# Seven block products instead of eight for gate and up in two of four feed-forwards of an fp32 encoder on one Trainium2 core

## The chip, the cores and the metric

One core of a Trainium2 chip runs the whole program. The metric is the device time of one execution in microseconds (us). The engines are TensorE (PE in the profile; PEld is its weight load), VectorE (DVE), ScalarE (ACT), GpSimd (POOL) and SyncE (SP), which issues the loads of weights.

## The reference

A trunk of two layers. Each layer is feed-forward, mixer, feed-forward, and every part is added to the residual x (512 tokens by 1024 features, float32):

```
x = x + 0.5 * swiglu(rms_norm(x, g1), w_gate, w_up, w_down)
x = x + mixer(rms_norm(x, g2))
x = x + 0.5 * swiglu(rms_norm(x, g3), w_gate, w_up, w_down)
swiglu(y) = (silu(y @ w_gate) * (y @ w_up)) @ w_down     # 1024 -> 2816 -> 1024
```

The change touches the first feed-forward (layer 0, before the mixer) and the last (layer 1, after it). The mixers (attention and a Fourier part in layer 0, latent attention and a state space part in layer 1) stay as they are.

## The kernel before

Activations lie transposed: x[c] holds features 128c to 128c+127 by 512 tokens, eight such tiles. Every fp32 operand of a product is split into a high and a low part in the type float32r (ScalarE copies the high part, VectorE subtracts it for the low part), and a product is the sum of three matmuls hi·hi, hi·lo and lo·hi (`mm3`, line 145; each is issued for 256 tokens at a time).

F = 2816 is 22 blocks of 128. A *unit* of weights is gate and up of one block: 128 partitions by 2048 columns, 1 MB, loaded by SP into one of three `raw` buffers (`load`), and split into `w_hi` (line 49, ScalarE) and `w_lo` (line 50, VectorE), two buffers each (`split`, `part`). A unit costs TensorE 8 feature blocks × 2 (gate, up) × 3 × 2 halves of the tokens = 96 matmuls of 128x128 by 256 columns, into the banks `pg` and `pu`. Behind it VectorE and ScalarE form the gate (lines 253 to 262): gn = pg · rows (255), sg = silu(gn) (257), un = pu · rows (259), a = sg · un (261), ah (154), al (161). `rows` holds each token's inverse root mean square, so that the norm is applied after the product; its columns come from squares of x by TensorE (`ms_cols`), a reciprocal root by Newton steps of 128x4 on VectorE (`rsqrt`, lines 205 to 218), and transposes on TensorE (`rows`). The down projection of 11 blocks at a time follows (two halves, `HF`), with one VectorE operation per chunk into x (line 298).

The tokens enter as `xg[c]`, x times the gain, split (`scale_split`), made chunk by chunk as the part before finishes x (`prep`). `side` is a generator of table operations (rope tables and others) of which one piece is emitted per unit.

The program is written unit by unit; a scheduler then fixes one static order per engine, and tiles from pools make a writer wait until the last reader of the buffer is done. Each engine works through its own list in order, so an operation that waits holds all that stand behind it in that list.

## Time and profile before

| what | value |
|---|---|
| median of 3 runs | 1852.09 us (1851.97 to 1856.15) |
| profiled execution | 1853.05 us, of which 1851.3 is the span of the trace |
| TensorE busy | 1830.1 us (99%), 15608 instructions |
| VectorE busy | 986.0 us (53%) |
| ScalarE busy | 622.6 us (34%) |

The span is the time from the first to the last instruction of the trace; the rest of the profiled execution lies around it. Busy shares are means over the whole program: what a stretch is bound by is read from that stretch.

### The profile page before, as it was taken

The page shows a single profiled execution, that of the slowest core. Times are in us where ns is not written, and L with a number is a line of the kernel's source. Part 1 is how long each engine was busy: PE and PEld are TensorE (multiplying, and loading weights), DVE is VectorE, ACT ScalarE, POOL GpSimd, SP SyncE. Part 2 cuts the span into 40 slices and gives each one's busy share as a digit, 9 for nine tenths or more (in the row PEclk, how much of TensorE's full clock was granted, in tenths as well). Part 3 has the DMA queues.
Part 4 walks back from the last instruction along what each step waited for, and adds up shares of the span by engine and source line. Part 5 has one row for each costly group of instructions (what it writes and reads, how often), then busy time and mean ns, then how long its engine had stood idle before and what let it go on. Part 6 is the DMA issues. An engine that isn't in the chain of part 4 may idle for free.

```text
span 1851.3 us, 35303 instructions
## 1 busy us (share of the span) xinstructions
PE 1830.1 (99%) x15608; PEld 1810.8 (98%) x15608; DVE 986.0 (53%) x1732; ACT 622.6 (34%) x818; POOL 85.4 (5%) x138
## 2 busy tenths in 40 slices
PE   9999999999999999999999999999989999999999
PEld 9999999999799999999999999999988899999999
DVE  5643444456955954556744434444688654434442
ACT  4321222324953222222332222223366632212321
POOL 0000000011120000000000000000045100000000
PEclk9999999999999999999999999999999999999999
DMA  6223221331122325342322233223144222133221
GB/s 209 93 73 121 95 105 64 117 108 68 37 92 92 113 100 150 112 111 100 128 103 92 79 116 110 89 73 109 69 129 141 79 96 103 64 118 113 85 89 67
DMA packets 63447, 185.65 MB, mean 100 GB/s; under 512 B 27424, under 2 KB 28352, under 8 KB 51136
## 3 DMA queue, kind: packets, MB, share of 16 engines
q1 hardware_dynamic: 63296, 183.41, 29.3%
q8 instruction: 122, 2.00, 0.4%
q14 instruction: 29, 0.24, 0.0%
HBM read 170.79 MB, written 10.49 MB: 98 GB/s over the span
## 4 chain that ended last, share of the span: by engine, by line
PE 95%; DVE 2%; ACT 1%; DMA 1%; issue 0%; POOL 0%; SPq 0%; ACTq 0%; POOLq 0%; DVEq 0%
PE pd L145 30%; PE pu L145 27%; PE pg L145 26%; PE pz L145 4%; PE etp L1447 1%; PE sc L145 1%; PE pf L145 1%; PE pql L145 1%; PE s_py L1230 1%; PE pq L145 1%; PE po L1467 0%; PE po L1468 0%; DVE et_lo L1459 0%; PE sc L533 0%; ACT e L1440 0%
## 5 line engine op out<-in xcount | busy, mean ns | idle before, releaser
L49 ACT ACTIVATE w_hi<-w_raw 128x2048 fp32r<-128x2048 f32 (+4 forms) x175 | 288.6, 1649 | 878.3 <-PE pu L145 449.7
L50 DVE TENSOR_TENSOR w_lo<-w_raw,w_hi 128x2048 fp32r<-128x2048 f32 (+4 forms) x172 | 338.2, 1966 | 166.2 <-ACT w_hi L49 166.0
L145 PE MATMUL pu<-xgh,w_hi 128*128 128x256 f32 x1440 | 282.9, 278 | 0.0
L145 PE MATMUL pu<-xgh,w_lo 128*128 128x256 f32 x1440 | 282.8, 278 | 0.0
L145 PE MATMUL pu<-xgl,w_hi 128*128 128x256 f32 x1440 | 282.6, 278 | 0.0
L145 PE MATMUL pg<-xgh,w_hi 128*128 128x256 f32 x1408 | 277.9, 279 | 1.2 <-ACT w_hi L49 1.2
L145 PE MATMUL pd<-al,w_hi 128*128 128x256 f32 x1408 | 277.5, 277 | 0.0
L145 PE MATMUL pd<-ah,w_lo 128*128 128x256 f32 x1408 | 277.4, 277 | 0.0
L145 PE MATMUL pd<-ah,w_hi 128*128 128x256 f32 x1408 | 276.7, 277 | 0.0
L145 PE MATMUL pg<-xgh,w_lo 128*128 128x256 f32 x1408 | 276.5, 278 | 0.0
L145 PE MATMUL pg<-xgl,w_hi 128*128 128x256 f32 x1408 | 276.4, 278 | 0.0
L145 PEld LDWEIGHTS pu<-xgh,w_hi 128*128 128x128 f32 x1440 | 218.7, 189 | 0.0
L145 PEld LDWEIGHTS pu<-xgh,w_lo 128*128 128x128 f32 x1440 | 218.2, 188 | 0.2 <-DVE w_lo L50 0.2
L145 PEld LDWEIGHTS pu<-xgl,w_hi 128*128 128x128 f32 x1440 | 218.2, 188 | 0.0
L145 PEld LDWEIGHTS pg<-xgh,w_hi 128*128 128x128 f32 x1408 | 213.8, 189 | 1.5 <-ACT w_hi L49 1.5
L145 PEld LDWEIGHTS pd<-ah,w_lo 128*128 128x128 f32 x1408 | 213.9, 188 | 0.0
L145 PEld LDWEIGHTS pd<-ah,w_hi 128*128 128x128 f32 x1408 | 213.6, 188 | 0.0
L145 PEld LDWEIGHTS pg<-xgl,w_hi 128*128 128x128 f32 x1408 | 213.4, 188 | 0.0
L145 PEld LDWEIGHTS pg<-xgh,w_lo 128*128 128x128 f32 x1408 | 213.4, 188 | 0.0
L145 PEld LDWEIGHTS pd<-al,w_hi 128*128 128x128 f32 x1408 | 213.4, 188 | 0.0
L255 DVE TENSOR_TENSOR gn<-pg,rows 128x512 f32<-128x512 f32 x88 | 60.7, 689 | 279.3 <-PE pg L145 279.3
L298 DVE SCALAR_TENSOR_TENSOR x<-pd,x 128x512 f32<-128x512 f32 (+1 forms) x65 | 44.4, 684 | 232.5 <-PE pd L145 232.5
(365 smaller groups left out, 2088.6 us busy)
## 6 DMA issues: line engine op xcount, KB each, us to landing
w_raw<-wa SPq DMA_DIRECT2D x86, 1024.0 KB, 4.9
w_raw<-wb SPq DMA_DIRECT2D x64, 704.0 KB, 4.0
w_raw<-we_qkv SPq DMA_DIRECT2D x6, 1024.0 KB, 4.9
w_raw<-we_out SPq DMA_DIRECT2D x3, 768.0 KB, 4.2
w_raw<-wo_out SPq DMA_DIRECT2D x3, 768.0 KB, 4.1
x<-xT SPq DMA_DIRECT2D x8, 256.0 KB, 5.5
dr_h<-s_h SPq DMA_DIRECT2D x8, 256.0 KB, 2.8
dr_g<-s_g SPq DMA_DIRECT2D x8, 256.0 KB, 3.0
```

The costliest lines, as they stand in the source:

```text
L49: self.nc.scalar.activation(hi, raw, AF.Copy)
L50: (self.eng or self.nc.vector).tensor_tensor(out=lo, in0=raw, in1=f32(hi), op=ALU.subtract)
L145: mm(out[:, c], lhs[l], rhs[r][:, c], start=first and i == 0 and j == 0, stop=last and i == 2, skip_group_check=len(cs) > 1)
L255: nc.vector.tensor_tensor(out=gn, in0=pg, in1=rstd, op=ALU.mult)
L298: nc.vector.scalar_tensor_tensor(out=x, in0=p, scalar=0.5, in1=x, op0=ALU.mult, op1=ALU.add)
L1230: nc.tensor.matmul(py[half][:, k, :], m[i][:, i4, :], r[:, k, :], start=i == 0, stop=i == 2)
L1447: nc.tensor.transpose(p[:, kc, :], e[:, kc * 128:kc * 128 + 128], T.ident)
```

## The change

Gate and up of a block are a product of a 256-column weight block (two halves of 128: gate and up) with 1024 features, and the tokens come in two halves of 256. Features are taken in two interleaved halves. So the product is a 2 by 2 block product: (gate, up) × (feature halves) × (token halves), eight block products. Strassen's scheme, in Winograd's form, gets by with seven, made from sums of weights and sums of tokens. A block product is here 4 feature blocks × 3 = 12 matmuls of 256 columns (`product`).

* Weights: g1 and g2 are the two halves of the gate's rows, u1 and u2 those of up's. The sums are s3 = g1 + u1 and s1 = u2 + u1 (one VectorE operation of 1024 columns, in place in `raw`), s2 = g1 + s1 and s4 = g2 + s2 (512 columns each); up comes out with its sign turned, which the -0.5 below sets right. g1, g2, s3, s1 lie in one tile of 2048 columns, which is split as before; s2, s4 and u2 are split apart (512 each). For this SP loads 1.5 MB per unit instead of 1 MB, in five pieces.
* Tokens: t1 to t4 are sums of the four blocks b11, b12, b21, b22, made once per feed-forward (`forms`), with two new copies with gain (y1, y2), and split.
* Order of a unit: g1·b11 (copied from the bank by ScalarE), s1·t1 (copied), then u2·t4 of the unit before it (copied, and its gate follows), s2·t2 accumulated on the first (copied), g2·b21, s4·b22, then gt's add on VectorE, s3·t3 accumulated (copied), and ut's add. Five bank copies of 256 columns by ScalarE and two adds by VectorE are new; `un` is gone: up's scale is applied behind the down projection, with the factor -0.5 (`rows` makes both).
* In the first feed-forward the first three of the 22 units stay as before, and t1 to t4 are made beside them. In the last feed-forward all 22 are new; t1 to t4 are made as the odd mixer finishes x (`prep_forms`).
* F is worked in three groups of 8, 7 and 7 blocks instead of two of 11, in these two feed-forwards; the chunk's addition into x is two VectorE operations.
* 60 slots of 512 columns become 66.

```diff
+GROUPS = (8, 7, 7)
...
     def load(self, i):
...
         raw = self.pool.tile([128, n], F32, tag="raw", name="w_raw", bufs=3)
-        for c in self.cuts(i, n):
-            self.nc.sync.dma_start(raw[:, c], src[:, c])
+        dma = self.nc.sync.dma_start
+        if slot:
+            self.u2[i] = slot("w_u2"), slot("w_u1")
+            dma(raw[:, 1024:1536], src[:, 0:512])
+            dma(raw[:, 1536:2048], src[:, 1536:2048])
+            dma(raw[:, 0:1024], src[:, 0:1024])
+            dma(self.u2[i][0], src[:, 1536:2048])
+            dma(self.u2[i][1], src[:, 1024:1536])
...
     def split(self, i):
...
+        if slot:
+            s = raw[:, 1024:2048].rearrange("p (a b) -> p a b", a=2)
+            self.nc.vector.tensor_tensor(out=s, in0=s, in1=self.u2[i][1][:, None, :].to_broadcast([128, 2, 512]), op=ALU.add)
         hi = self.pool.tile([128, n], F32R, tag="hi", name="w_hi")
         lo = self.pool.tile([128, n], F32R, tag="lo", name="w_lo")
         for c in self.cuts(i, n):
             self.part(raw[:, c], hi[:, c], lo[:, c])
-        self.ready[i] = (hi, lo)
+        self.ready[i] = self.forms(i, raw, hi, lo, slot) if slot else (hi, lo)
+    def forms(self, i, raw, hi, lo, slot):
+        add = self.nc.vector.tensor_tensor
+        out = {n: (hi[:, o:o + 512], lo[:, o:o + 512]) for n, o in (("g1", 0), ("g2", 512), ("s3", 1024), ("s1", 1536))}
+        s2, s4 = slot("w_s2"), slot("w_s4")
+        add(out=s2, in0=raw[:, 0:512], in1=raw[:, 1536:2048], op=ALU.add)
+        add(out=s4, in0=raw[:, 512:1024], in1=s2, op=ALU.add)
+        for n, f in (("s2", s2), ("s4", s4), ("u2", self.u2.pop(i)[0])):
+            out[n] = slot(n + "h", F32R), slot(n + "l", F32R)
+            self.part(f, *out[n])
...
+    def forms(self, j, norm, plain=None):
+        nc, v = self.nc, self.nc.vector
...
+        y1, y2 = self.slot("y1"), self.slot("y2")
+        for i, y in enumerate((y1, y2)):
+            g = norm * KD + 2 * j + i
+            nc.scalar.activation(y, self.x[2 * j + i], AF.Copy, scale=self.gains[:, g:g + 1])
+        b11, b12, b21, b22 = y1[:, 0:256], y1[:, 256:512], y2[:, 0:256], y2[:, 256:512]
+        ta, tb = self.slot("ta"), self.slot("tb")
+        t1, t2, t3, t4 = ta[:, 0:256], ta[:, 256:512], tb[:, 0:256], tb[:, 256:512]
+        v.tensor_tensor(out=t1, in0=b11, in1=b12, op=ALU.subtract)
+        v.scalar_tensor_tensor(out=t2, in0=t1, scalar=-1.0, in1=b22, op0=ALU.mult, op1=ALU.subtract)
+        v.tensor_tensor(out=t3, in0=b22, in1=b12, op=ALU.subtract)
+        v.scalar_tensor_tensor(out=t4, in0=t2, scalar=-1.0, in1=b21, op0=ALU.mult, op1=ALU.subtract)
+        if plain:
+            p1, p2 = plain
+        else:
+            q = self.slot("b1", F32R, (128, 2, 256))
+            nc.scalar.activation(q[:, 0], b11, AF.Copy)
+            v.tensor_tensor(out=q[:, 1], in0=b11, in1=f32(q[:, 0]), op=ALU.subtract)
+            p1, p2 = (q[:, 0], q[:, 1]), self.split(y2, "b2")
+        pa, pb = self.split(ta, "ta"), self.split(tb, "tb")
...
+    def product(self, out, w, n, first, last):
+        for k in range(KD // 2):
+            x = self.tf[n][k]
+            for i, (l, r) in enumerate(((0, 0), (0, 1), (1, 0))):
+                self.nc.tensor.matmul(out, w[l][:, k * 128:k * 128 + 128], x[r], start=first and k == 0 and i == 0,
+                                      stop=last and k == 3 and i == 2, skip_group_check=True)
+    def ffn_s(self, after, side=iter(()), plain=0, norm=0, ends=False):
...
+        def finish(sg_in, up):
+            gn = self.slot("gn")
+            tt(out=gn, in0=sg_in, in1=st["rows"], op=ALU.mult)
+            nc.scalar.activation(gn, gn, AF.Silu)
+            h = self.slot("a")
+            if up[1]:
+                nc.vector.scalar_tensor_tensor(out=h, in0=gn, scalar=-1.0, in1=up[0], op0=ALU.mult, op1=ALU.mult)
+            else:
+                tt(out=h, in0=gn, in1=up[0], op=ALU.mult)
+            act.append(self.split(h, "a"))
...
+        def last_product(u):
...
+            self.product(pb[:, a], w["u2"], "t4", False, True)
+            nc.scalar.activation(ut[:, a], pb[:, a], AF.Copy)
+            wait.append((gt, (ut, False)))
+            flush()
+        def unit(prev):
+            w = self.W.next()
+            pb, pc = self.bank("pg"), self.bank("pu")
+            gt, ut = self.slot("gt"), self.slot("ut")
+            copy = nc.scalar.activation
+            self.product(pb[:, a], w["g1"], "b11", True, False)
+            copy(gt[:, a], pb[:, a], AF.Copy)
+            self.product(pc[:, b], w["s1"], "t1", True, False)
+            copy(ut[:, a], pc[:, b], AF.Copy)
+            last_product(prev)
+            self.product(pb[:, a], w["s2"], "t2", False, False)
+            copy(gt[:, b], pb[:, a], AF.Copy)
+            self.product(pc[:, a], w["g2"], "b21", False, True)
+            self.product(pc[:, b], w["s4"], "b22", False, True)
+            tt(out=gt, in0=gt, in1=pc, op=ALU.add)
+            self.product(pb[:, a], w["s3"], "t3", False, False)
+            copy(ut[:, b], pb[:, a], AF.Copy)
+            tt(out=ut[:, b], in0=ut[:, b], in1=ut[:, a], op=ALU.add)
+            return {"w": w, "pb": pb, "gt": gt, "ut": ut}
...
+                if plain and f <= plain:
+                    for j in ((), (0,), (1, 2, 3))[f - 1]:
+                        self.forms(j, norm, (self.xg[2 * j], self.xg[2 * j + 1]))
...
+                def out(c, p, ts=slice(0, S)):
+                    t, x = self.slot("dn")[:, ts], self.x[c][:, ts]
+                    tt(out=t, in0=p, in1=st["down"][:, ts], op=ALU.mult)
+                    tt(out=x, in0=x, in1=t, op=ALU.add)
...
-    T.ffn_units(0, 1)
+    T.ffn_s_units(0, 1, 3)
...
-    T.ffn_units(1, 2)
+    T.ffn_s_units(1, 2)
     T.start(0)
-    T.ffn(prep(1), tables(), 1)
+    T.ffn_s(prep(1), tables(), 3)
...
-    T.odd_mixer(prep(5))
-    T.ffn(None, ends=True)
+    T.odd_mixer(lambda c: T.prep_forms(c, 5))
+    T.ffn_s(None, ends=True)
```

What the scheduler makes of it, at three places.

Place 1, VectorE in the first feed-forward, from the subtraction behind the reciprocal root, before (a gate of one pending unit, then the next unit's):

```order
L50 TENSOR_TENSOR w_lo_580<-w_raw_430,w_hi_579 128x2048
L255 TENSOR_TENSOR gn_541<-pg_169,rows_539 128x512
L259 TENSOR_TENSOR un_545<-pu_170,rows_539 128x512
L261 TENSOR_TENSOR a_547<-sg_543,un_545 128x512
L161 TENSOR_TENSOR al_551<-a_547,ah_549 128x512
L255 TENSOR_TENSOR gn_553<-pg_303,rows_539 128x512
```

The same place in the change (w_lo_681 is the low part of the second converted unit; gn to al belong to the three plain units; ta and tb hold the token sums t1, t2 and t3, t4, tal and tbl their low parts):

```order
L63 TENSOR_TENSOR w_lo_681<-w_raw_454,w_hi_680 128x2048
L405 TENSOR_TENSOR gn_590<-pg_169,rows_586 128x512
L409 SCALAR_TENSOR_TENSOR a_593<-gn_590,pu_170 128x512
L189 TENSOR_TENSOR al_597<-a_593,ah_595 128x512
L405 TENSOR_TENSOR gn_599<-pg_309,rows_586 128x512
L409 SCALAR_TENSOR_TENSOR a_602<-gn_599,pu_310 128x512
L189 TENSOR_TENSOR al_606<-a_602,ah_604 128x512
L405 TENSOR_TENSOR gn_608<-pg_483,rows_586 128x512
L409 SCALAR_TENSOR_TENSOR a_611<-gn_608,pu_484 128x512
L189 TENSOR_TENSOR al_615<-a_611,ah_613 128x512
L239 TENSOR_TENSOR ta_621<-y1_617 128x256
L240 SCALAR_TENSOR_TENSOR ta_621<-ta_621,y2_618 128x256
```

Before, the gates of pending units were followed by nothing that TensorE needs at once; in the change the token sums of the second pair (ta_621) stand behind all three gates.

Place 2, VectorE in the middle of the first feed-forward, before (one unit's whole list):

```order
L255 TENSOR_TENSOR gn_1218<-pg_1120,rows_539 128x512
L259 TENSOR_TENSOR un_1222<-pu_1121,rows_539 128x512
L50 TENSOR_TENSOR w_lo_1233<-w_raw_1114,w_hi_1232 128x2048
L261 TENSOR_TENSOR a_1224<-sg_1220,un_1222 128x512
L161 TENSOR_TENSOR al_1228<-a_1224,ah_1226 128x512
```

in the change (it makes the sums s2 and s4, and gt_2131 is the add to a bank copy):

```order
L464 TENSOR_TENSOR gt_2131<-gt_2131,pu_2130 128x512
L411 TENSOR_TENSOR a_2175<-gn_2172,ut_1999 128x512
L63 TENSOR_TENSOR w_lo_2243<-w_raw_2100,w_hi_2242 128x2048
L467 TENSOR_TENSOR ut_2132<-ut_2132 128x256
L189 TENSOR_TENSOR al_2179<-a_2175,ah_2177 128x512
L81 TENSOR_TENSOR w_s2_2246<-w_raw_2100 128x512
L69 TENSOR_TENSOR w_raw_2233<-w_raw_2233,w_u1_2235 128x1024
L82 TENSOR_TENSOR w_s4_2247<-w_raw_2100,w_s2_2246 128x512
L63 TENSOR_TENSOR s2l_2251<-w_s2_2246,s2h_2250 128x512
L63 TENSOR_TENSOR s4l_2255<-w_s4_2247,s4h_2254 128x512
L63 TENSOR_TENSOR u2l_2259<-w_u2_2101,u2h_2258 128x512
```

and ScalarE there, which had one w_hi, one silu and one ah per unit (gt and ut are copies from the banks pg and pu; s2h, s4h and u2h the high parts of the weight sums; pg_2129 belongs to one unit, pg_2262 to the next):

```order
L406 ACTIVATE gn_2172<-gn_2172 128x512
L62 ACTIVATE w_hi_2242<-w_raw_2100 128x2048
L466 ACTIVATE ut_2132<-pg_2129 128x256
L182 ACTIVATE ah_2177<-a_2175 128x512
L446 ACTIVATE ut_2132<-pg_2129 128x256
L62 ACTIVATE s2h_2250<-w_s2_2246 128x512
L62 ACTIVATE s4h_2254<-w_s4_2247 128x512
L62 ACTIVATE u2h_2258<-w_u2_2101 128x512
L456 ACTIVATE gt_2264<-pg_2262 128x256
L458 ACTIVATE ut_2265<-pu_2263 128x256
```

The bank copy gt_2264 now stands behind s2h, s4h and u2h in ScalarE's list, and those wait for VectorE's sums, which stand behind w_lo_2243.

Place 3, ScalarE at the start of the last feed-forward, before (x5 to x7 are the last chunks that the odd mixer's output is added to; w_hi belongs to units of weights):

```order
L154 ACTIVATE xgh_17175<-x5_79,gains_70 128x512
L195 ACTIVATE sqc_17179<-x5_79 128x512
L49 ACTIVATE w_hi_17283<-w_raw_17183 128x2048
L154 ACTIVATE xgh_17264<-x6_80,gains_70 128x512
L195 ACTIVATE sqc_17268<-x6_80 128x512
L154 ACTIVATE xgh_17273<-x7_81,gains_70 128x512
L195 ACTIVATE sqc_17277<-x7_81 128x512
L49 ACTIVATE w_hi_17416<-w_raw_17281 128x2048
```

and in the change (y1 and y2 are x6 and x7 times the gain, b1 and b2h the high parts of their blocks):

```order
L62 ACTIVATE s2h_17685<-w_s2_17681 128x512
L62 ACTIVATE s4h_17689<-w_s4_17682 128x512
L62 ACTIVATE u2h_17693<-w_u2_17544 128x512
L258 ACTIVATE sqc_17772<-x6_80 128x512
L62 ACTIVATE w_hi_17815<-w_raw_17668 128x2048
L258 ACTIVATE sqc_17777<-x7_81 128x512
L235 ACTIVATE y1_17781<-x6_80,gains_70 128x512
L235 ACTIVATE y2_17782<-x7_81,gains_70 128x512
L247 ACTIVATE b1_17791<-y1_17781 128x256
L182 ACTIVATE b2h_17794<-y2_17782 128x512
```

The fourth pair's y1, y2 and b1 now stand behind the high parts of three weight sums and the next unit's w_hi.

## Rows read from the trace of the kernel before

**Rows 1.** The page: span, busy times by engine, and the chain's shares.

```profile
span 1851.3 us, 35303 instructions
...
PE 1830.1 (99%) x15608; PEld 1810.8 (98%) x15608; DVE 986.0 (53%) x1732; ACT 622.6 (34%) x818; POOL 85.4 (5%) x138
...
PE 95%; DVE 2%; ACT 1%; DMA 1%; issue 0%; POOL 0%; SPq 0%; ACTq 0%; POOLq 0%; DVEq 0%
```

**Rows 2.** TensorE's waits, 0 to 450 and 1430 to 1851: sum, count, longest.

```profile
PE pg L145 <- ACT w_hi L49: 1.2, 1, 1.2
...
PE pglu L145 <- ACT s_zh L154: 1.5, 1, 1.5
```

**Rows 3.** Window 200 to 250: PE, PEld, DVE, ACT, POOL, clock, DMA, GB/s.

```profile
200.00:250.00 50.00, 50.00 (x443) 50.00 (x443) 21.90 (x23) 14.72 (x14) 0.00 (x0) 1.00 0.27 97
```

**Rows 4.** The chain in order of time: start, us, what, matmuls.

```profile
133.25 59.84 PE pd L145 x528
```

**Rows 5.** Timeline of TensorE near the end: start, duration, operation.

```profile
1842.14 0.28 PE L145 MATMUL pd<-ah,w_hi 128*128 128x256 f32 x1
1842.25 0.28 PE L145 MATMUL pd<-al,w_hi 128*128 128x256 f32 x1
1842.37 0.28 PE L145 MATMUL pd<-ah,w_lo 128*128 128x256 f32 x1
```

**Rows 6.** Groups by form, VectorE: busy us, mean ns, idle before.

```profile
L50 DVE TENSOR_TENSOR w_lo<-w_raw,w_hi 128x2048 fp32r<-128x2048 f32 x95 | 217.8, 2292 | 125.5 <-ACT w_hi L49 125.5
...
L50 DVE TENSOR_TENSOR w_lo<-w_raw,w_hi 128x1024 fp32r<-128x1024 f32 x4 | 4.9, 1224 | 1.3 <-ACT w_hi L49 1.3
...
L175 DVE SCALAR_TENSOR_TENSOR v<-pz,rs_y,v 128x256 fp32r<-128x256 f32 x8 | 3.9, 482 | 3.7 <-ACT v L174 3.7
...
L796 DVE TENSOR_TENSOR knat<-kp,rs_y 128x256 f32<-128x256 f32 x8 | 3.3, 413 | 0.0
```

**Rows 7.** Groups by form, ScalarE.

```profile
L257 ACT ACT_TABLE_LOAD x3 | 3.8, 1283 | 0.1
L174 ACT ACTIVATE v<-pz,rs_y 128x256 fp32r<-128x256 f32 x8 | 3.8, 471 | 4.3 <-PE pz L145 2.3 <-DVE v L175 2.0
...
L235 ACT ACTIVATE rows<-rows 128x512 f32<-128x512 f32 x5 | 2.9, 582 | 0.3 <-PE rows L233 0.3
```

**Rows 8.** Timeline of VectorE, 44 to 51, first gates of the program.

```profile
44.50 2.29 DVE L50 TENSOR_TENSOR w_lo<-w_raw,w_hi 128x2048 fp32r<-128x2048 f32 x1 [8.84 <-ACT w_hi L49]
46.71 0.68 DVE L255 TENSOR_TENSOR gn<-pg,rows 128x512 f32<-128x512 f32 x1
47.31 0.68 DVE L259 TENSOR_TENSOR un<-pu,rows 128x512 f32<-128x512 f32 x1
...
49.48 0.69 DVE L161 TENSOR_TENSOR al<-a,ah 128x512 fp32r<-128x512 f32 x1 [0.70 <-ACT ah L154]
50.09 0.68 DVE L255 TENSOR_TENSOR gn<-pg,rows 128x512 f32<-128x512 f32 x1
```

**Rows 9.** Timeline of ScalarE before the last feed-forward.

```profile
1477.85 1.92 ACT L49 ACTIVATE w_hi<-w_raw 128x2048 fp32r<-128x2048 f32 x1 [2.73 <-issue]
1479.67 0.71 ACT L154 ACTIVATE xgh<-x,gains 128x512 fp32r<-128x512 f32 x1
1480.28 0.62 ACT L195 ACTIVATE sqc<-x 128x512 f32<-128x512 f32 x1
1480.80 0.71 ACT L154 ACTIVATE xgh<-x,gains 128x512 fp32r<-128x512 f32 x1
```

**Rows 10.** DMA issues (KB, us to landing); window 9 to 10.

```profile
w_raw<-wa SPq DMA_DIRECT2D x86, 1024.0 KB, 4.9
...
9.00:10.00 1.00, 1.00 (x6) 1.00 (x6) 1.00 (x2) 0.96 (x3) 0.00 (x0) 1.00 1.07 410
```

**Rows 11.** Windows of 5 us in the odd mixer; granted clock third from last.

```profile
1350.00:1355.00 5.00, 5.00 (x24) 5.00 (x24) 2.89 (x11) 3.88 (x11) 0.00 (x0) 0.50 0.23 53
...
1390.00:1395.00 5.00, 3.46 (x19) 3.03 (x18) 2.80 (x7) 2.50 (x6) 4.70 (x4) 0.72 0.87 262
```

More of the change, by code (lines that the diff above doesn't have):

```diff
@@ L17 @@
 HF = NF // 2
+GROUPS = (8, 7, 7)
 HT = S // 2 + 2
 EPS = 1e-6
+SCRATCH = 4096
 def f32(ap):
@@ L30, in __init__, with add @@
         self.nc, self.pool, self.eng = nc, pool, None
-        self.units, self.raw, self.ready = [], {}, {}
+        self.units, self.raw, self.ready, self.u2 = [], {}, {}, {}
         self.pos = self.loaded = self.cut = 0
-    def add(self, src, n):
-        self.units.append((src, n))
+    def add(self, src, n, slot=None):
+        self.units.append((src, n, slot))
     def load(self, i):
-        src, n = self.units[i]
+        src, n, slot = self.units[i]
         raw = self.pool.tile([128, n], F32, tag="raw", name="w_raw", bufs=3)
-        for c in self.cuts(i, n):
-            self.nc.sync.dma_start(raw[:, c], src[:, c])
+        dma = self.nc.sync.dma_start
[7 more added lines that the diff above has]
+        else:
+            for c in self.cuts(i, n):
+                dma(raw[:, c], src[:, c])
         self.raw[i] = raw
@@ L190, in scale_split, with prep_forms @@
         self.xg[c] = self.split(self.x[c], "xg", g)
+    def prep_forms(self, c, norm, b=None):
+        self.square(c)
+        if c % 2 == 1:
+            self.forms(c // 2, norm)
+    def forms(self, j, norm, plain=None):
+        nc, v = self.nc, self.nc.vector
+        if j == 0:
+            self.tf = {n: [None] * 4 for n in ("b11", "b21", "b22", "t1", "t2", "t3", "t4")}
+        y1, y2 = self.slot("y1"), self.slot("y2")
[17 more added lines that the diff above has]
+        pa, pb = self.split(ta, "ta"), self.split(tb, "tb")
+        a, b = slice(0, 256), slice(256, 512)
+        for n, p, c in (("b11", p1, a), ("b21", p2, a), ("b22", p2, b), ("t1", pa, a), ("t2", pa, b), ("t3", pb, a), ("t4", pb, b)):
+            self.tf[n][j] = tuple(z[:, c] for z in p)
     def square(self, c):
@@ L226, in small, with rows @@
         return lambda n, dt=F32: self.tiny.tile([128, w], dt, tag=f"{n}{w}", name=n)
-    def rows(self, col):
+    def rows(self, col, scale=None):
         nc = self.nc
@@ L235, in rows @@
         nc.scalar.activation(r, p, AF.Copy)
-        return r
+        if scale is None:
+            return r
+        rs = self.slot("rows")
+        nc.scalar.activation(rs, p, AF.Copy, scale=scale)
+        return r, rs
     def ffn_units(self, l, which):
@@ L302, in ffn, with ffn_s_units @@
                     after(c)
+                next(side, None)
+    def ffn_s_units(self, l, which, plain=0):
+        wa, ws, f = self.t[f"wa{which}"], self.t[f"ws{which}"], 0
+        for g, n in enumerate(GROUPS):
+            for i in range(n):
+                if f < plain:
+                    self.W.add(wa[l, f], 2048)
+                else:
+                    self.W.add(ws[l, f], 2048, self.slot)
+                f += 1
+            for j in range(KD // 2):
+                self.W.add(self.t[f"wd{which}_{g}"][l, j], 2 * n * 128)
@@ L1616, in layout @@
         dn = g(f"ffn{w}_w_down").reshape(2, 2, HF, 128, KD, 128).transpose(0, 1, 4, 3, 2, 5)
+        gs = gu.reshape(2, NF, 128, 4, 2, 2, 128).transpose(0, 1, 2, 5, 4, 3, 6)
+        out[f"ws{w}"] = gs.reshape(2, NF, 128, 2048)
+        f = 0
+        for i, n in enumerate(GROUPS):
+            dg = g(f"ffn{w}_w_down").reshape(2, NF, 128, 4, 2, 128)[:, f:f + n].transpose(0, 3, 2, 4, 1, 5)
+            out[f"wd{w}_{i}"] = dg.reshape(2, 4, 128, 2 * n * 128)
+            f += n
         out[f"wb{w}"] = dn.reshape(2, 2, KD, 128, HF * 128)
```

89 lines of the change are left out of this document (85 added, 4 removed).

## The prediction

> **What bounds the kernel now.** I read the page first, its busy shares and the shares of its chain: TensorE works 1830.1 of 1851.3 us and carries 95% of the chain that ended last, VectorE 53%, ScalarE 34% [rows 1]. So a matmul saved in a dense stretch is its spacing saved, as long as nobody else falls behind. Is the stretch dense? The idle times before instructions, for the first and the last feed-forward, show one wait on a weight copy, 1.2 us at the program's start, and in the last 420 us only two of 1.5 us, both in the odd mixer, of which one is shown [rows 2]. In a 50 us window of the first feed-forward TensorE works all 50.00 us, VectorE 21.90, ScalarE 14.72 [rows 3]. So today the others have slack of more than half. The spacing of matmuls: the chain holds several undisturbed runs of 528 in 59.84 us, 0.1133 us each [rows 4]; the timeline of the last ones shows starts 0.11 to 0.12 apart though one lasts 0.28 [rows 5]. What follows a matmul therefore has its result about 0.17 us after the next one has started.
>
> **Removed.** In a converted unit 7 products of 12 matmuls (84) stand for 96. 19 + 22 = 41 units are converted (three of the first feed-forward's 22 stay): 492 matmuls, × 0.1133 = **−55.8 us**. A unit then lasts 9.52 us on TensorE instead of 10.88.
>
> **Added on VectorE.** Prices by form: 2048 columns 2.292 us, 1024 1.224, 256 0.413 (0.482 with two operations) [rows 6], and 512 0.68 to 0.69 [rows 8]. They pipeline a little: the large subtraction starts at 44.50 and the next operation at 46.71, 512-column ones follow each other 0.60 to 0.61 apart [rows 8]; I take spacings 2.21, 1.14, 0.61, 0.34. A unit before: 2.21 + 4 × 0.61 = 4.65. Now: add of 1024, 1.14; low part 2.21; nine of 512 (s2, s4, three low parts, gt's add, gn, a, al), 5.49; ut's add 0.34: **9.2 us** against TensorE's 9.52. Full durations give 10.1. ScalarE: a copy of 2048 lasts 1.92 (spacing 1.82), 512-column ones start 0.52 apart [rows 9]; a unit has one of 2048, three of 512, silu and ah, and five bank copies of 256 columns. A plain copy of 256 from a bank stands nowhere; one scaled by a row's factor took 0.471, a plain one of 512 from a bank 0.582 [rows 7], so it lies between 0.3 (half of that) and 0.47; I take 0.38. ScalarE comes to 6.3 us and is no bound by itself.
>
> So VectorE has 0.3 us of slack per unit if it never waits. It does: each gate chain gn, silu, a, ah, al holds a hole of 0.70 us before al [rows 8], which was free and now isn't unless the scheduler fills it. 9.2 + 0.70 = 9.9 and one more hand-over of the same kind gives 10.6: about 1 us over TensorE per unit. Bounds: 0 (holes filled) and 1.9 (full durations and 1.3 us of holes).
>
> **A wait, step by step.** Bank copies stand between products: the unit's second product in pb may not begin before ScalarE has copied the first. In the order shown as place 2, that copy (gt_2264) stands behind s2h, s4h and u2h, which wait for VectorE's sums, which stand behind the large subtraction. From the end of the product that frees the hi buffer: result 0.21, w_hi 1.92, hand-over 0.03, w_lo 2.21, ut 0.34, al 0.61, s2 0.61, the next unit's add 1.14, s4 0.69, hand-over 0.04, s4h and u2h 0.53 each, the copy 0.38, hand-over 0.04: **9.3 us**. TensorE has until there 56 matmuls, 6.3 us, and waited 0.3 for w_lo: **2.6 us** of wait. I walked both programs' orders in this way, with these prices on each row; for the program before, it gives no wait in these stretches, as the trace shows.
>
> **First feed-forward, first group: +32 us.**
> (a) 2.6: the 15 small operations of the reciprocal root stand among eight large sums, and the fourth unit waits for the transposes behind it.
> (b) 18.3, the largest single term. As place 1 shows, three pending gates and then the token sums of pairs 1 to 3 stand behind w_lo_681 on VectorE. A gate chain repeats after 3.39 us (gn at 46.71, the next at 50.09 [rows 8]); before, two full units hid them. Now every second product needs t1 of all pairs, and TensorE has 30 matmuls, 3.4 us, without it. What TensorE waits for is w_lo (2.21, mostly run by then), the table load 1.28 [rows 7], 3 gates 10.2, three pairs at about 3.0 each (two copies with gains in turn with four sums and two splits) 9.0, then the copy for s2, against 3.4 + 18 matmuls trickling in: 9.4 + 2.3 + 2.3 + 3.1 and 1.2 of small waits.
> (c) 11.2 in the rest: 4.4 and 1.0 on the next w_hi, 4.9 on a w_lo that stands behind the small operations of the rope tables, 0.9 of crumbs.
> **Groups two and three: +13.0** (6.7 and 6.3, waits as above: 2.5, 1.2 to 2.0, 1.0 and crumbs).
>
> **Start of the last feed-forward: +17.1 us.** Before, x's gain, square and split are one unit's rows [rows 9] and nothing waits. Now (place 3): the last but one residual add at T0 lets VectorE do the add of 1024 and ScalarE w_hi, to T0 + 4.0, and w_lo to T0 + 6.8; TensorE has few matmuls left and waits 3.3, then 2.4. The fourth pair's b1 stands on ScalarE behind s2h, s4h (which wait for VectorE to T0 + 9.9), u2h, a square, the next w_hi, a square, y1, y2: 9.9 + 0.53 + 0.53 + 0.74 + 1.82 + 3 × 0.53 + 0.42 = T0 + 15.5, where TensorE has run out at 8.4: 7.2. Then 0.9, 0.2, and 3.2 for s2's copy behind the second unit's forms.
> **Groups of the last feed-forward: +23.1** (9.6, 6.8, 6.7). With the 13.0 above that is 36.1 over some 36 units, the 1 us per unit of the balance.
> **Down projection: +0.7.** Two VectorE operations per chunk take 1.2 us and hide under the next chunk's matmuls (7 × 3 × 2, 4.8 us), except in the last half, where one more of 256 columns and a hand-over stand at the end.
> **DMA: 0.** 1.5 MB per unit instead of 1. 1024 KB land in 4.9 us alone, and the start moved 410 GB/s [rows 10]; 1.5 MB in 9.5 us is 166 GB/s. What hides it is the three raw buffers, two units ahead; at half of 410 GB/s 7.7 us per unit would still do.
> **Clock: +6.** After a gap of 1.94 us at 1387 the window 1390 to 1395 shows a granted clock of 0.72 [rows 11], 5 × 0.28 = 1.4 us lost; four gaps above 4 us, 5.6.
>
> Sum: −55.8 + 32.1 + 13.0 + 17.1 + 23.1 + 0.7 + 5.6 = **+35.8**. On the profiled span 1851.3 that is 1887.1; 1.75 outside the span and −0.96 between the profiled execution and the median give 1888. I forecast **1887 us**.
>
> **Rivals.**
> *1, faster: the groups' waits vanish.* VectorE's work (9.2) is below TensorE's (9.52); if buffers let the holes fill, the 36.1 us go, and the clock's loss shrinks to 1: −55.8 + 32.1 + 17.1 + 0.7 + 1 = −4.9, **1847**. It decides where the waits fall below (55.8 − 50.9)/36 = 0.14 us per unit. For it: the order gives steady patterns. Against: bank copies sit behind VectorE-fed copies in ScalarE's row. Chance 0.10.
> *2, VectorE holds each operation its full duration* where operands alternate between engines: 10.1 instead of 9.2 per unit, 0.5 more over 41 units: **1907**. For it: 0.689 is the duration; against: 0.61 is the spacing shown. Chance 0.14. The Trainium skill, "VectorE: DVE Perf Modes", section "The DRAIN you can't avoid", says that the next operation does not start until the pipe is empty; the rows here show starts 0.08 us before the end, so the trace does not quite bear it out.
> *3, TensorE loses clock at every gap.* In 1350 to 1355, after a stretch of short gaps, it worked 5.00 us at a granted clock of 0.50, the 1.2 GHz level, for 24 matmuls [rows 11]: 2.5 us per gap. Ten gaps of over 1.8 us: 25 instead of 5.6, **1907**. Chance 0.12. The Trainium skill, "TensorE: Matmul & The Clock Gate", Part 1, has half rate as the state to which an idle engine falls back, which those windows agree with; how many of these gaps set it off no row tells.
> *4, transfers late.* Five DMAs per unit from SP, of rows a half to a fourth as long as those that landed in 4.9 us [rows 10]. If a unit's raw came 3 us late at each of the four starts of groups after the first: **1899**. Chance 0.05.
>
> **Numbers.** Main case 0.57 (1872 to 1900: the copy price, 0.3 to 0.47 for five copies in a chain, and the small waits move it by 12 either way), rival 2 0.14, 3 0.12, 4 0.05, rival 1 0.10, no change 0.02. The range leaves out rival 1 and the far tail of 2 and 3: 1862 to 1912. 0.3%, 5.6 us, is what a measurement of this kernel tells from no change: faster 0.09 (most of rival 1, whose own price is 4.9), same 0.04, slower 0.87.
>
> **What would show it.** TensorE's waits in the first 120 us: about 18 us on tah/tal and s2h, 4 to 5 on a w_lo; in the groups waits on s2h copies of 1 to 2.6 us, VectorE over 90% busy there; 17 us of waits at the start of the last feed-forward, before the second product. If VectorE is below 90% in the groups and TensorE has no waits, rival 1 is right; if the matmuls are longer than 0.113 apart with no wait, rival 3. I am wrong altogether if TensorE does not run in the order's sequence against ScalarE's copies as I walked it.

## The result, and the profile after

The change makes the kernel slower: 1905.44 us median (1904.53 to 1909.51) against 1852.24 in the same comparison, ratio 1.0286, 95% interval 1.0266 to 1.0307. The forecast was 1887, with 1862 to 1912 as its range. So the sign was right and the time lies inside the range, 18 us above the forecast; what the time is made of was not as forecast, as the rest shows.

The page of the changed kernel (span, busy times, shares of the chain), beside [rows 1]:

```profile
span 1902.8 us, 35440 instructions
...
PE 1827.8 (96%) x15116; PEld 1799.2 (95%) x15116; DVE 1225.3 (64%) x2121; ACT 774.6 (41%) x1172; POOL 85.6 (4%) x138
...
PE 81%; DVE 7%; ACT 5%; DMA 4%; issue 2%; SPq 1%; POOL 0%; DVEq 0%; ACTq 0%; POOLq 0%
```

492 instructions are gone from TensorE, as counted, but the chain no longer runs on TensorE alone. TensorE's waits, in us, number and longest, beside [rows 2], up to 460 us and then from 1470 us on:

```profile
PE pu L390 <- ACT tah L182: 10.1, 3, 8.0
PE pg L390 <- ACT gt L456: 9.2, 6, 2.3
PE pg L390 <- ACT w_hi L62: 4.3, 2, 2.4
```
```profile
PE pg L390 <- ACT gt L456: 12.5, 9, 2.6
PE pg L390 <- ACT w_hi L62: 7.0, 3, 3.2
PE pg L390 <- ACT b L247: 5.5, 1, 5.5
```

They are where the forecast put them: the token sums (tah), the bank copy ahead of s2's product (gt), the next unit's w_hi, and b1 at the start of the last feed-forward. Now the windows (columns as in [rows 3]): the stretch of the gates and token sums, the first down projection, the second group, and the start of the last feed-forward.

```profile
40.00:85.00 45.00, 27.87 (x165) 25.41 (x164) 35.68 (x73) 25.19 (x42) 0.00 (x0) 0.73 0.26 88
...
125.00:165.00 40.00, 40.00 (x342) 40.00 (x341) 22.58 (x26) 8.44 (x8) 0.00 (x0) 1.00 0.42 142
165.00:240.00 75.00, 71.04 (x580) 70.24 (x580) 58.39 (x74) 39.92 (x69) 0.00 (x0) 0.98 0.34 120
...
1515.00:1540.00 25.00, 13.98 (x76) 12.72 (x76) 24.57 (x46) 13.79 (x21) 0.00 (x0) 0.66 0.27 84
```

The second of these rows is the surprise. TensorE is busy all of the 40 us, at full clock, in a down projection that the change hardly touches, and it does 342 matmuls: 0.117 us each. The chain says it more exactly, beside [rows 4]:

```profile
125.77 39.70 PE pd L173 x337
```

39.70 / 337 is 0.1178 us, where the same matmuls took 0.1133 before. To size this I took the start times of all 256-column matmuls in the trace and sorted the steps from one to the next: steps above 0.13 us at full clock, and those above 0.26 us in stretches where the granted clock was 0.50, are waits; the shorter steps in those stretches go under clock, each less 0.1133; of the others what exceeds 0.1133 is spacing (a step with a missing record counts as two). "Other" is the small matmuls between.

```
                     matmuls x 0.1133   waits   clock   spacing   other    sum (us)
first ffn, before         357.2          0.3     0.0      3.0      1.5     362.0
first ffn, after          331.4         34.6     8.9     12.5      1.5     388.9
last ffn, before          358.7          0.2     0.0      0.9      1.2     361.0
last ffn, after           329.7         33.1     5.6     13.8      2.1     384.3
```

So the first feed-forward is 26.8 us longer and the last 23.3: saved 54.8, waits +67.2, clock +14.5, wider spacing +22.4, other +0.9; 1.3 us more lie between the two.

### The profile page after: what moved, and what is told of

The parts are those of the page before. It is cut to its first block, busy times and chain, and to the rows that moved or that the text cites. A ratio compares the mean times of both kernels' runs of the same rounds, so it can differ in the third digit from the quotient of the medians.

```text
span 1902.8 us, 35440 instructions
## 1 busy us (share of the span) xinstructions
PE 1827.8 (96%) x15116; PEld 1799.2 (95%) x15116; DVE 1225.3 (64%) x2121; ACT 774.6 (41%) x1172; POOL 85.6 (4%) x138
## 4 chain that ended last, share of the span: by engine, by line
PE 81%; DVE 7%; ACT 5%; DMA 4%; issue 2%; SPq 1%; POOL 0%; DVEq 0%; ACTq 0%; POOLq 0%
PE pd L173 29%; PE pu L173 13%; PE pg L173 13%; PE pg L390 8%; PE pu L390 6%; PE pz L173 4%; DMA w_u<-ws 2%; ACT w_hi L62 2%; DVE w_lo L63 1%; PE etp L1673 1%; PE pql L173 1%; PE pf L173 1%; DMA w_raw<-ws 1%; DVE w_raw L69 1%; ACT e L1666 1%
## 5 line engine op out<-in xcount | busy, mean ns | idle before, releaser
L62 ACT ACTIVATE w_hi<-w_raw 128x2048 fp32r<-128x2048 f32 (+6 forms) x167 | 286.8, 1717 | 658.2 <-PE pu L173 211.5
L63 DVE TENSOR_TENSOR w_lo<-w_raw,w_hi 128x2048 fp32r<-128x2048 f32 (+5 forms) x164 | 336.8, 2053 | 140.8 <-ACT w_hi L62 139.8
L173 PE MATMUL pu<-xgh,w_hi 128*128 128x256 f32 x784 | 154.7, 279 | 0.0
L173 PE MATMUL pu<-xgl,w_hi 128*128 128x256 f32 x784 | 154.4, 278 | 0.0
L173 PE MATMUL pu<-xgh,w_lo 128*128 128x256 f32 x784 | 154.4, 279 | 0.0
L173 PE MATMUL pg<-xgh,w_hi 128*128 128x256 f32 x752 | 149.3, 280 | 0.8 <-ACT w_hi L62 0.8
L173 PE MATMUL pg<-xgl,w_hi 128*128 128x256 f32 x752 | 148.1, 278 | 0.0
L173 PE MATMUL pg<-xgh,w_lo 128*128 128x256 f32 x752 | 148.1, 278 | 0.0
L173 PEld LDWEIGHTS pu<-xgl,w_hi 128*128 128x128 f32 x784 | 119.0, 188 | 0.0
L173 PEld LDWEIGHTS pg<-xgh,w_hi 128*128 128x128 f32 x752 | 114.7, 189 | 1.1 <-ACT w_hi L62 1.1
```

What stands on the lines that cost most here:

```text
L62: self.nc.scalar.activation(hi, raw, AF.Copy)
L63: (self.eng or self.nc.vector).tensor_tensor(out=lo, in0=raw, in1=f32(hi), op=ALU.subtract)
L173: mm(out[:, c], lhs[l], rhs[r][:, c], start=first and i == 0 and j == 0, stop=last and i == 2, skip_group_check=len(cs) > 1)
```

## Experiments

The first four tell apart the parts of the change and two ideas on the waits. Each ratio is to the kernel before, measured beside that run on the same chip.

**The groups alone.** `T.ffn_s_units(0, 1, 3)` and the calls that belong to it get 22 for 3, in the last feed-forward too, so that no unit is converted:

```diff
-    T.ffn_s(prep(1), tables(), 3)
+    T.ffn_s(prep(1), tables(), 22)
...
-    T.ffn_s(None, ends=True)
+    T.ffn_s(None, plain=22, norm=5, ends=True, sq=False)
```

> All 22 units of both feed-forwards stay plain (eight block products, 96 matmuls); groups of 8, 7 and 7, the two VectorE operations per chunk, the scale behind the down projection and the 66 slots stay as in the change. If the spacing of 0.1178 us in the changed feed-forwards comes from interruptions of TensorE, there are few of them here: spacing 0.113 in most of both feed-forwards as before, no waits in the groups, 1852 to 1857 us. If it comes from the new layout (groups, slots, two banks per pair of chunks), the spacing is 0.1178 here too: about 2940 matmuls x 0.0045 us in each of two feed-forwards, 1868 to 1876 us.

Measured 1852.87 us, ratio 0.9995 (0.9986 to 1.0005). The chain has `pd` at 0.1133:

```profile
220.15 38.08 PE pd L173 x336
```

Three groups, two operations per chunk and the moved scale cost nothing; layout is out, and the wider spacing belongs to the converted units.

**The last feed-forward alone**, the first as before:

```diff
-    T.ffn_s_units(0, 1, 3)
+    T.ffn_units(0, 1)
...
-    T.ffn_s(prep(1), tables(), 3)
+    T.ffn(prep(1), tables(), 1)
```

> First feed-forward as before, last one changed. In the changed kernel's trace the first feed-forward is 26.8 us longer than before and the last 23.3. If the two parts are independent: 1852 + 24 = 1876 us, with the last feed-forward's waits (33 us) as in the change. If one part burdens the other (transfers, the level of the spacing handed on through the program), the result is off that by more than 5 us.

Measured 1880.19 us, ratio 1.0143 (1.0123 to 1.0163): 4 us above the sum and inside its 5, with waits of 35.1 us and 9.2 for the clock where the full change had 33.1 and 5.6. The two feed-forwards pay on their own.

**Token sums ahead of the gates** in the first feed-forward:

```diff
+                if plain and f <= plain:
+                    for j in ((0,), (1,), (2, 3))[f - 1]:
+                        self.forms(j, norm, (self.xg[2 * j], self.xg[2 * j + 1]))
                 stats()
                 flush()
-                if plain and f <= plain:
-                    for j in ((), (0,), (1, 2, 3))[f - 1]:
```

> In the first feed-forward the token sums of pair 0 are written at the first plain unit, pair 1 at the second, pairs 2 and 3 at the third, ahead of the three pending gates. If the gates ahead of the token sums are the cost of that stretch, its 8.4 + 1.5 + 1.5 + 2.8 us of waits go to some 4 and the kernel comes to 1890 to 1894 us, the lower clock there included. If the stretch is short of VectorE and ScalarE time as such, the wait only moves behind the gates (on the copy ahead of s2) and the kernel stays at 1900 to 1906.

Measured 1901.5 us, ratio 1.0258 (1.0237 to 1.0279). The wait only moved. The longest was 8.0 on tah; now the longest is as long, on the bank copy that stands behind the gates:

```profile
PE pg L390 <- ACT gt L456: 20.2, 11, 7.9
PE pu L390 <- ACT rows L302: 5.5, 1, 5.5
```

So the order of gates and token sums alone is not the cost. Three gates, three pairs of token sums and two units' weight sums want VectorE and ScalarE at once there; that these are short of time as such, as the second expectation has it, is not shown: from 40 to 85 us VectorE is busy for 34.4 and ScalarE for 23.2 of the 45 us in this run.

**VectorE with a fifth less to do per unit**:

```diff
-            out[n] = slot(n + "h", F32R), slot(n + "l", F32R)
-            self.part(f, *out[n])
+            hi = slot(n + "h", F32R)
+            self.nc.scalar.activation(hi, f, AF.Copy)
+            out[n] = hi, hi
```

> The low parts of s2, s4 and u2 are left out (their high parts are used in their place, so these products are coarser): three VectorE operations of 512 columns fewer per converted unit, 1.8 us of 9.2. If VectorE's total work sets the waits in groups two and three, they vanish there (9.5 us in the first feed-forward, 9.3 in the last) and the kernel comes to about 1880 us. If the chain through the hi buffer (last product that reads it, w_hi, w_lo, sums, ScalarE's list, bank copy) sets them, they stay at 4 to 5 us per group of seven units, in other places, and the kernel comes to 1890 to 1900 us.

The high part stands in the low part's place too, so the largest of the three products is counted twice and the result is not merely coarser: this kernel is a probe of time alone. Measured 1893.29 us, in a single execution, so without an interval. In the same sorting of steps the second and third groups wait 2.6 and 3.8 us in the first feed-forward and 4.8 and 2.4 in the last, against 5.1, 5.9, 6.1 and 5.0 in the change: some 60% of the waits outlast the work. Neither expectation holds cleanly; total work is a part of it at most.

**The sum of 1024 columns on GpSimd**, to take it off VectorE for good:

```diff
-            self.nc.vector.tensor_tensor(out=s, in0=s, in1=self.u2[i][1]...
+            self.nc.gpsimd.tensor_tensor(out=s, in0=s, in1=self.u2[i][1]...
```

> The in-place sum of 1024 columns (s3 and s1) is made by GpSimd, everything else as in the change. GpSimd took 2.4 us for a subtraction of 1032 columns in the kernel before, and has nothing else to do here; VectorE loses 1.14 us per unit, which stood in the chain of the waits before s2's product. If that chain sets them, the waits of 2.4 us in the groups and part of those at both starts go, about 20 us in all: 1885 us. If GpSimd and VectorE hinder each other when they work side by side (VectorE's 512-column operations longer than 0.69 us), the kernel stays at 1900 or goes above 1905.

Measured 1950.37 us, ratio 1.0512 (1.0491 to 1.0533). Groups by form, first GpSimd's over the span:

```profile
L69 POOL TENSOR_TENSOR w_raw<-w_raw,w_u 128x1024 f32<-128x1024 f32 x41 | 111.0, 2712 | 590.8 <-DMA w_u<-ws 377.1 <-DVE x L502 69.4 <-DVE w_lo L63 59.0
```

then VectorE's row of al up to 400 us, in this kernel and, in the second fence, in the changed one:

```profile
L189 DVE TENSOR_TENSOR al<-a,ah 128x512 fp32r<-128x512 f32 x22 | 21.5, 976 | 12.6 <-ACT ah L182 12.4
```
```profile
L189 DVE TENSOR_TENSOR al<-a,ah 128x512 fp32r<-128x512 f32 x22 | 15.2, 690 | 10.7 <-ACT ah L182 10.7
```

An operation of 0.69 us took 0.98 on average. In VectorE's operations of 512 columns that belong to weights and gates, all eight up to 420 us that took over 0.9 us ran beside a GpSimd sum. The Trainium skill, "SBUF — State Buffer", section "Who interferes with whom", says that a VectorE instruction with two inputs in SBUF contends with a GpSimd instruction that reads SBUF; these rows agree. How much of the 45 us over the change comes from this, and how much from the sum itself, which took 2.71 us where VectorE needed 1.22, this run does not separate.

**First groups plain, and weight parts in one pair of tiles.** Two runs, and one with both and the GpSimd sum. In the first, `plain` is 8 in both feed-forwards and the token sums are made one pair per unit (`{3: (0,), 4: (1,), 5: (2,), 6: (3,)}`). In the second (54 slots left):

```diff
-        hi = self.pool.tile([128, n], F32R, tag="hi", name="w_hi")
-        lo = self.pool.tile([128, n], F32R, tag="lo", name="w_lo")
+        m = n + 1536 * bool(slot)
+        hi = self.pool.tile([128, m], F32R, tag="hi", name="w_hi")
+        lo = self.pool.tile([128, m], F32R, tag="lo", name="w_lo")
...
-        for n, f in (("s2", s2), ("s4", s4), ("u2", self.u2.pop(i)[0])):
-            out[n] = slot(n + "h", F32R), slot(n + "l", F32R)
+        for o, n, f in ((2048, "s2", s2), (2560, "s4", s4), (3072, "u2", self.u2.pop(i)[0])):
+            out[n] = hi[:, o:o + 512], lo[:, o:o + 512]
```

> The first group (8 units) of both feed-forwards stays plain, the token sums are made one pair per unit beside the fourth to seventh unit; 28 units are converted, 336 matmuls fewer than before, 38.1 us. The waits of both starts and first groups go (24 and 21 us of 67); each later group keeps its 4.7 to 5.9, 21 in all; half clock behind the waits above 2 us some 6. With the spacing at 0.1178 from the first interruption on, 2 x 1850 x 0.0045 = 16.6: 1852 - 38.1 + 21 + 6 + 16.6 = 1858 us. If the spacing is set by the long waits of the first group, it stays at 0.113: 1842.

> High and low parts of s2, s4 and u2 lie in the same two tiles as those of g1, g2, s3 and s1 (3584 columns) and not in slots; 54 slots instead of 66. In the changed kernel a matmul with weights from these slots is 0.120 us from the next, and at 344.86 and 104.66 us the spacing goes from 0.113 to 0.120 and then 0.1178 at the first of them, without a wait. If weights in the slots beside the tokens cause this, the spacing falls to 0.113 in most of both feed-forwards, 22 us less, and with the waits that the new order has by my reckoning (12 us fewer): 1871 us. If interruptions alone set the level, only the waits differ: 1893 us.

> First groups plain, the sum of 1024 columns on GpSimd, all weight parts in one pair of tiles. 336 matmuls fewer, 38.1 us; by the order and the rows of this case waits of 0.6 us at three units per group, 7 in all. If weights in slots set the spacing, it stays at 0.113: 1852 - 38.1 + 7 + 2 = 1823 us. If interruptions do, 16.6 on top: 1839 us. If GpSimd hinders VectorE, the waits of the groups stay: 1855 us.

Plain first groups: 1863.46 us, ratio 1.0037 (1.002 to 1.0054), 5 above the first expectation. The waits of the starts are gone, each later group keeps 6.1 to 6.2, and the spacing is wide from 148.96 us on but for short stretches: long waits at the start don't cause it. One pair of tiles: 1877.24, ratio 1.0118 (1.0098 to 1.0138). Its waits are about as long as in the change (65.5 us), but the spacing costs 2.9 and 0.4 us instead of 12.5 and 13.8. With nearly the same waits and an eighth of the spacing cost, interruptions alone don't set the level: where the weights lie matters. The weight parts have left the slots here too, and the later groups still wait some 4 us each, at other places, for `w_lo` and for the copy ahead of u2's product. All three together: 1848.36, ratio 0.9967 (0.9951 to 0.9983), held back by GpSimd (VectorE's u2 low part took 1.15 us there).

**Who has to leave the ring of slots.** The slots are one ring of tiles of 512 columns, from which token parts, gates, bank copies, loads of u1 and u2, weight sums and their parts are all taken. The weight parts get a ring of their own (first diff, 54 slots left), the same with plain first groups, and, as a cross-check, the loads instead (second diff, 60 slots left):

```diff
-            out[n] = slot(n + "h", F32R), slot(n + "l", F32R)
+            out[n] = tuple(self.pool.tile([128, 512], F32R, tag="form", name=n + c, bufs=12) for c in "hl")
```
```diff
-            self.u2[i] = slot("w_u2"), slot("w_u1")
+            self.u2[i] = tuple(self.pool.tile([128, 512], F32, tag="load", name=c, bufs=6) for c in ("w_u2", "w_u1"))
```

> High and low parts of s2, s4 and u2 come from a ring of their own (12 tiles of 512 columns, as large as slots), 54 slots stay for the rest; all 41 units converted. If the waits in the groups come from the one ring of slots, in which a part of a weight sum waits for the release of whatever stood there before, the waits in the second and third groups (10 us in each feed-forward) go and those of the starts shrink: by the order and the rows of this case some 35 us fewer, 1870 us. If they come from VectorE's and ScalarE's amount of work, which is the same, it stays at 1900. On top: if the spacing of 0.1178 comes from weights that lie in the slots beside the tokens, it is 0.113 here and 22 us more go, 1848 us; if it comes from weights in tiles of 512 columns, it stays.

> The ring of their own for the weight parts, and the first group of 8 units plain in both feed-forwards, token sums beside them; 28 units converted. By the order and the rows no wait of TensorE is left in either feed-forward: 1852 - 38.1 + 1 = 1815 us with the spacing at 0.113, 1832 us with 0.1178 from the first converted unit on. If VectorE's amount of work is the limit after all, waits of 5 us per group stay: 1835 to 1852 us.

> The loaded blocks w_u1 and w_u2 come from a ring of their own (6 tiles), 60 slots stay for the rest, the weight parts among them; all 41 units converted. In the changed kernel VectorE waits 6.7 us for loads of w_u in the two feed-forwards, in the kernel with a ring for the weight parts not at all. If late loads cause the waits in the groups, they go here as there, 1870 to 1885 us, with the wider spacing. If the weight parts in the ring of slots cause them, by keeping the slots behind them back, fewer slots make it worse: by the order and the rows 24 us more, 1925 to 1930 us.

Own ring for the weight parts: 1850.73 us, ratio 0.998 (0.9964 to 0.9996), 57 us of the change's cost gone with not one operation fewer. In the sorting of steps about 31 of them are waits, 20 spacing (6.8 us are left of the change's 26.3) and the rest clock. Window of the second group, and the chain's first down projection:

```profile
165.00:240.00 75.00, 75.00 (x661) 74.83 (x661) 60.48 (x80) 40.88 (x69) 0.00 (x0) 1.00 0.38 127
```
```profile
121.71 38.19 PE pd L173 x337
```

TensorE works all 75 us and does 661 matmuls where the change did 580; VectorE does the same kind of work, at 81%. Waits in the four later groups: 0.2, 0.1, 0.2 and 0.1 us. With plain first groups besides: 1819.82 us, ratio 0.9815 (0.9793 to 0.9837), the fastest version; TensorE has no wait of note in either feed-forward. With the loads in a ring of their own: 1922.85, ratio 1.0362 (1.0324 to 1.04), near what was expected if the weight parts cause the waits; the waits in its later groups are 6.6 to 8.8 us. But this run can't tell the two readings apart, since it did not take late loads away. VectorE waited for pieces of `w_raw` before almost every sum of 1024 columns, where in the change it waited 6.7 us for `w_u`:

```profile
DVE w_raw L69 <- DMA w_raw<-ws: 76.0, 38, 3.6
```

In its second group the chain runs through such loads, of 4.1 to 4.6 us each. In the change the chain runs through no transfer in three of the four later groups, and through two loads in the last, while the longest wait is the same in all four (2.3 us): that is what speaks against late loads as the cause there.

What differs in the order can be read from the timelines at place 2, VectorE's first. The change:

```profile
197.27 2.29 DVE L63 TENSOR_TENSOR w_lo<-w_raw,w_hi 128x2048 fp32r<-128x2048 f32 x1 [1.88 <-ACT w_hi L62]
...
200.42 0.68 DVE L81 TENSOR_TENSOR w_s<-w_raw 128x512 f32<-128x512 f32 x1
...
202.16 0.68 DVE L82 TENSOR_TENSOR w_s<-w_raw,w_s 128x512 f32<-128x512 f32 x1
```

and the kernel with the ring for the weight parts:

```profile
187.99 0.69 DVE L81 TENSOR_TENSOR w_s<-w_raw 128x512 f32<-128x512 f32 x1
188.71 0.69 DVE L82 TENSOR_TENSOR w_s<-w_raw,w_s 128x512 f32<-128x512 f32 x1
189.43 2.29 DVE L63 TENSOR_TENSOR w_lo<-w_raw,w_hi 128x2048 fp32r<-128x2048 f32 x1
```

The sums s2 and s4 (L81, L82) stand behind `w_lo` in the one and ahead of it in the other. ScalarE, in the change:

```profile
195.32 1.92 ACT L62 ACTIVATE w_hi<-w_raw 128x2048 fp32r<-128x2048 f32 x1 [1.75 <-PE pg L390]
...
201.13 0.63 ACT L62 ACTIVATE s2h<-w_s 128x512 fp32r<-128x512 f32 x1 [0.75 <-DVE w_s L81]
202.87 0.63 ACT L62 ACTIVATE s4h<-w_s 128x512 fp32r<-128x512 f32 x1 [1.11 <-DVE w_s L82]
203.41 0.61 ACT L62 ACTIVATE u2h<-w_u 128x512 fp32r<-128x512 f32 x1
203.93 0.36 ACT L456 ACTIVATE gt<-pg 128x256 f32<-128x256 f32 x1
```

and the kernel with the ring for the weight parts:

```profile
187.48 1.92 ACT L62 ACTIVATE w_hi<-w_raw 128x2048 fp32r<-128x2048 f32 x1
...
189.56 0.62 ACT L62 ACTIVATE s2h<-w_s 128x512 fp32r<-128x512 f32 x1
190.08 0.37 ACT L456 ACTIVATE gt<-pg 128x256 f32<-128x256 f32 x1
...
190.61 0.64 ACT L62 ACTIVATE s4h<-w_s 128x512 fp32r<-128x512 f32 x1
```

In the second the sums are ready when w_hi ends, and the bank copy comes before s4h and u2h: 2.6 us from w_hi's start to the copy's, where the change needs 8.6. In the later groups of the change no operation that writes a weight sum or part into a slot waited for TensorE; s2h and s4h waited for VectorE's sums, 23.8 and 5.7 us in all. So what delays the copy at run time is its place in the lists, as far as the trace tells, and not a slot that is still being read.

**One matmul** added to the kernel before, at the head of the second half of each feed-forward:

```diff
             act = []
+            if h == 1:
+                w = self.xg[0][0]
+                nc.tensor.matmul(self.bank("probe")[:, 0:256], w[:, 0:128], w[:, 0:256], start=True, stop=True)
```

> The kernel before with one matmul more (128x128 by 256) at the head of the second half of each of the four feed-forwards, its weights and its moving data both from slots, its result unused. Its own cost is 4 x 0.12 us. If weights in slots set the level of the spacing and the level then stays, the 1584 matmuls of the second half run at 0.1178 instead of 0.113 in the three feed-forwards where they ran at 0.113: 3 x 7 = 21 us, 1873 us. If the level isn't set by such a matmul, 1852.5 us.

Measured 1872.89 us, ratio 1.01 (1.0079 to 1.0121). Four matmuls of 0.12 us cost 18.5 us. The chain, down projections of the first and second half of the first feed-forward, 528 matmuls each, and below them the second half in the kernel before:

```profile
131.72 59.84 PE pd L145 x528
316.05 62.19 PE pd L145 x528
```
```profile
312.77 59.84 PE pd L145 x528
```

Before, the second half has the spacing of the first ([rows 4]). In the three feed-forwards that ran at the narrow level there, the wide one begins at the added matmul (191.40, 1122.28 and 1679.61 us) and holds to the end of the half. So one matmul whose weights and moving data lie in a slot can set the level. A matmul at the same place with weights from elsewhere was not run; that any added matmul would do it is thus not excluded by this run alone.

## Why the prediction held, and where it did not

*Removed, −55.8: right.* The trace has the 492 matmuls fewer (15608 and 15116); the sorting gives −54.8 for them at 0.1133, since 8 fall to steps that it books elsewhere.

*Waits, +85.3: places right, too large.* They are +67.2. By groups, in us:

```
            first ffn: group 1   2     3      last ffn: start and group 1   2     3
predicted              32.1     6.7   6.3                    26.7          6.8   6.7
measured               23.6     5.1   5.9                    22.0          6.1   5.0
own ring               21.8     0.2   0.1                    14.6          0.2   0.1
```

The wait worked out step by step as 9.3 us of chain and 2.6 of wait is in the rows above: from w_hi at 195.32 to the copy's end at 204.29 it is 9.0 us, where the same steps of the forecast make 9.0 too, and the wait is 2.3 (a step of 2.45 from one matmul to the next). Terms (b) and the start of the last feed-forward were 2 to 5 us too large, and in (c) the w_lo behind the rope tables waited 0.5 and not 4.9.

*The balance of VectorE, 9.9 to 10.6 us per unit against TensorE's 9.52, as the reason for about 1 us of group waits per unit: this step failed.* The walk through the order had the right places and nearly the right waits; its sum of 36.1 us met the balance by chance. The waits sit at three units of a group and not at all units, VectorE stood idle 1.88 us before w_lo at place 2 and was busy 78% there and not over 90, some 60% of the waits outlast a fifth less work, and with a ring of their own for the weight parts they vanish at the same work. They come from where bank copies and sums stand in the lists, and the place in the lists changes with the ring: that is shown by the run with a ring for the weight parts. Leaving the slots is not enough by itself, as the run with one pair of tiles shows, and the run with the loads in their own ring brought late loads of its own. Why the scheduler writes the lists the one way or the other is not settled.

*Rival 1*, in which the group waits vanish, was thus within reach: not in this program, but with 12 tiles moved. That its 1847 us and the 1850.73 of that run lie so close is luck: the run still has 37 us of waits in the first groups, where rival 1 has 49, and it pays for clock and spacing what rival 1 does not. *Rival 2* fell: spacings on VectorE are as in [rows 8] (`w_lo` to the next 2.21, 512 columns 0.60). *Rival 3* was half right: the clock cost 14.5 us and not 5.6. In 40 to 85 the mean granted clock was 0.73 and in 1515 to 1540 0.66; behind the series of waits there TensorE worked at the 1.2 GHz level, which four gaps at 1.4 us undercount. The sign given for it, matmuls more than 0.113 us apart without a wait, did turn up, but at a granted clock of 1.00: it pointed to the spacing below and not to the clock. *Rival 4:* VectorE waited 6.7 us for loads of w_u in the two feed-forwards, little of it in the later groups (1.4 us). In the first group of the last feed-forward, though, the chain runs through four of these loads, 24.8 of the 43 us from 1538 to 1581:

```profile
1538.33 5.72 DMA w_u<-ws
1550.59 6.70 DMA w_u<-ws
1561.13 6.58 DMA w_u<-ws
1575.45 5.80 DMA w_u<-ws
```

So the forecast's 0 for transfers does not hold there; what they cost apart from the other waits of that group, no run separates.

*Spacing 0.1133 for all matmuls: the term that was missing, +22.4 us.* The forecast read it from runs of `pd` in [rows 4, 5] and took it as the price of a matmul. Three of the change's seven products take weights from slots, and the steps of them and of most of what follows are wider. That the place of the weights has a part in it is shown by the two runs that moved them; what exactly sets the level stays open, as the last section tells.

So the span's +51.5 us (1902.8 less 1851.3) against the +35.8 of the sum is: waits 18.1 too large and the tail's 0.7, clock 8.9 too small, spacing missing with 22.4, and 3.2 in the matmuls counted, the other matmuls and what lies between the two feed-forwards. Two errors of about 20 us with opposite signs brought the forecast as near as it came.

## What to carry to other kernels

Where a saving on the bound engine is 3%, its price per instruction must be checked in more than one stretch: two levels 4% apart stood in the trace of before. When the lists of an order interleave badly, look at which buffers share a ring before counting work; here the same work ran without a wait in the later groups once six tiles per unit had a ring of their own. And leave the first group of a stage plain, so that what the new scheme needs to begin is made beside matmuls that don't need it: that, with the ring, turned +2.9% into −1.9%.
